# Seeding the fourth product's PSUM bank with a ScalarE copy of the first, and keeping the up-projection's weight sums in DRAM, in a one-layer convolution, scan and MLP trunk

## The chip, the cores and the metric

The kernel runs on one core of a Trainium2 chip. The time is what the device needs for one execution, in microseconds (us). Three runs of the kernel before gave a median of 2695.03 us (2694.9 to 2701.88). Five engines take part, each with an instruction stream of its own: TensorE (PE, with its weight loads listed as PEld), VectorE (DVE), ScalarE (ACT), GpSimd (POOL) and SyncE (SP). SP's stream issues nearly all of the kernel's transfers, one after the other. An engine works through its stream in order: an instruction that waits holds up whatever stands behind it.

## The reference

One layer works on x of shape (1, 2048, 1024) in float32. A normalisation and one input projection feed two mixers, a gated short convolution and a Mamba-2 state-space scan (SSD); an output projection and a squared-ReLU MLP with residual sums follow, then a last normalisation.

```python
h = rmsnorm(x, norm_mix_w)
proj = jnp.einsum("btd,dc->btc", h, w_in)
u_b, u_c, u_h, z, xbc, dt_raw = jnp.split(proj, SPLITS, axis=-1)
y_a = short_conv_mixer(u_b, u_c, u_h, short_conv_w)        # u_b * conv3(u_c * u_h)
y_b = ssd_mixer(z, xbc, dt_raw, ...)                       # conv4, silu, chunked scan, gate silu(z), rmsnorm
x = x + jnp.einsum("btc,cd->btd", jnp.concatenate([y_a, y_b], axis=-1), w_out)
h = rmsnorm(x, norm_mlp_w)
hid = jnp.square(jax.nn.relu(jnp.einsum("btd,df->btf", h, w_up)))
return x + jnp.einsum("btf,fd->btd", hid, w_down)
```

## The kernel before

**Three matmuls for one product.** Operands are float32. Each is split into a high part in the matmul format (`whi`, `uh`: a cast on ScalarE, L100 and L315) and the rest (`wlo`, `ul`: a subtraction on VectorE, L101 and L316). A product of 128x128 weights and 128x512 activations is three matmuls: high by high, high weights by low activations, low weights by high activations (L270, L271, L272).

**Seven products for eight.** The input projection, the MLP's up-projection and the down-projection multiply 2x2 blocks in the manner of Strassen and Winograd. A block multiplication is a *chain* (`Seven.chain`, L244 to L281) of seven products, in the order of the table `PRODUCTS`: b11, t1, t2, b21, t3, b22, t4. Each sums over four *places* (pieces of the contraction), so it is 12 matmuls, and a chain has 84. Activations stand ready as sums and differences of their blocks, split into high and low. The weights need three forms besides the first block: `s12` and `s34` (two halves each), formed on VectorE by four 128x512 additions or subtractions (`combine`, L223 to L242; they appear as L231 and L208), and the last block `a22`.

**Banks.** A product's result grows in a PSUM bank of 128x512. A chain has three by name: `px` takes b11 and, on top of it, t2, t3 and t4, each of which continues the sum (`start=False`); `py` takes t1 and then b22; `pw` takes b21 alone. `accs` sets how many buffers each kind has: 3 for px and py and 1 for pw in the projection, 4 and 2 in the MLP and the down-projection (L1533). After each product `evict` reads what the result needs: b11 alone belongs to the block c11 = b11 + b21, so before the change px is copied aside after b11 by ScalarE (`s1`, L689 in the projection, L835 in the MLP), and VectorE adds it to pw after b21 (`add`, L692 and L838). t1 and t2 are put aside in the same way (`s5`, `s2`) and added to what t3 and b22 give. While a copy of px is outstanding, t2 may not write on px.

**The stages.** Times are those of the trace.
- Input projection (`Proj`), first half of the positions: a start until about 200 us, then 20 chains until about 478 us. A pair of output columns has a kind: `z` (Silu on the result), `b` (multiplied by the convolution `cc`), `ch` and `x` (kept for the convolutions). This half forms the weight sums and stores `s12` and `s34` to DRAM (L234, L240). Its second half, about 478 to 965 us, has 22 chains, loads most of the sums from DRAM instead of forming them, and runs the scan on the side; the scan's instructions stand between those of the chains (L1206 to L1271).
- Output projection (`Output`), about 965 to 1411 us: 64 units of plain products; L1427 adds the residual. In its last units the MLP's first activations are loaded and split (`settle`, L314 to L316).
- MLP (`Mlp`), 16 chains on each half of the positions, about 1419 to 1742 us and to 2043 us. Each half loads the two weight blocks of a chain, `r0` and `r1` (512 KB each, tag `wraw`), and forms the sums anew. `relu2` (L841, L842) is a Relu and a Square on ScalarE; `store` writes the activations that the down-projection will need to `hid_d`.
- Down-projection (`down`, L953 to L981), about 2043 to 2640 us: chains listed in `STEPS`, one or two groups each, 35 groups in all. Every product is added on VectorE to an accumulator `acc` in SBUF (L969), which starts as the residual loaded from `x1_d`. `refill` loads the hidden activations back (`rh`) and splits them.
- The last three blocks and the norm, to the end.

**What sets the order.** The kernel is built with the Tile framework. Its scheduler decides in which order each engine's instructions stand; the code gives dependences, buffers and a sequence of calls. `chain` takes the next chain's weights from a generator `ahead`, one step after each product named in it, so that casts and sums for the next chain stand between the evictions of this one. Tags with a number of buffers (`wraw` 3, `whi` and `wlo` 4, `us` 2) decide how early a load or a split may begin.

Of the kernel before, what the change touches and what calls it, by code (L numbers as in the profile page):

```python
# [11 lines left out]
F32 = mybir.dt.float32  # L12
F32R = mybir.dt.float32r
AF = mybir.ActivationFunctionType
ALU = mybir.AluOpType

P = 128
# [6 lines left out]
KD = D // P  # L24
# [15 lines left out]
def trunk(ctx: ExitStack, tc: tile.TileContext, x, w_in, w_dt, w_out, w_up, w_down, cvec, hrow, out):  # L40
# [9 lines left out]
    accs = {}  # L50
# [139 lines left out]
    class Seven:  # L190
# [53 lines left out]
        def chain(self, groups, ws, ahead, evict, after):  # L244
# [3 lines left out]
            got = []  # L248
            PRODUCTS = (
                ("b11", 0, 0, "x", 1),  # L250
                ("t1", 1, 0, "y", 1),
                ("t2", 1, 1, "x", 0),
                ("b21", 0, 1, "w", 1),
                ("t3", 2, 0, "x", 0),
                ("b22", 2, 1, "y", 0),
                ("t4", 3, 0, "x", 0),
            )
            for name, wn, half, acc, first in PRODUCTS:
                at = half * n
                for gi, g in enumerate(groups):  # L260
                    if first:
                        tag = "mw" if acc == "w" else "mm"
                        pm[gi][acc] = psum(tag, "p" + acc, accs[tag])
                    p = pm[gi][acc]
                    i, j = WHERE[name]
                    for k, place in enumerate(g):
                        hi, lo = (t[:, (at + k) * P : (at + k + 1) * P] for t in ws[wn])
                        h = [t[:, j] for t in place[i]]
                        kw = dict(skip_group_check=not first)
                        nc.tensor.matmul(p, hi, h[0], start=bool(first and k == 0), stop=False, **kw)  # L270
# [3 lines left out]
                for gi in range(len(groups)):  # L274
                    evict(name, gi, pm[gi])
# [5 lines left out]
            return got  # L281

# [106 lines left out]
    class Proj(Seven):  # L389
# [272 lines left out]
        def pair(self, h, what, ws, ahead, after):  # L662
# [31 lines left out]
            def evict(name, gi, pm):  # L694
                if name == "b11":
                    copy(pm["x"], "s1")
# [4 lines left out]
                elif name == "b21":  # L701
                    add("c11", pm["w"], "s1")
# [6 lines left out]
                elif name == "b22":  # L709
                    add("c12", pm["y"], "s2")  # L710
                    if kind == "z":
                        nc.scalar.activation(a, a, AF.Silu)
                        nc.sync.dma_start(sz_d[h][:, n], a)
                    elif kind == "b":
                        mul(a, a, self.cc[n])
# [27 lines left out]
        def weights(self, h, what):  # L743

            if h == 0:
                sums_d[what] = dram.tile([P, 2, 1024], F32, name=f"sums_{what}_d")
                raws = self.load_cols(w_in, self.cols(what))()
                yield
                yield from self.combine(*raws, sums_d[what])
                return  # L750
            f0, f1 = self.cols(what)
            raw = lambda n, w=1024: wp.tile([P, 1024], F32, tag="wraw", name=n, bufs=3)[:, 0:w]
            r0 = load_w(w_in[f0])
            if what not in sums_d:
                r1 = load_w(w_in[f1])
                yield
                yield from self.combine(r0, r1)
                return
            s12, s34 = raw("s12"), raw("s34")
            nc.sync.dma_start(s12, sums_d[what][:, 0])  # L760
# [837 lines left out]
```

## Time and profile before

| what | value |
|---|---|
| median of three runs | 2695.03 us (2694.9 to 2701.88) |
| the profiled execution's span | 2694.2 us |
| what lies around the span, against the median | 0.8 us |
| TensorE busy | 2610.2 us, 12024 matmuls |
| VectorE busy | 1979.4 us, 2687 instructions |
| ScalarE busy | 1381.7 us, 2042 instructions |
| data moved | 522.27 MB, mean 194 GB/s |

By stage, TensorE's busy time is 277.6 of 278 us between 200 and 478 us (first half of the projection), 479.9 of 487 us in its second half, 431.2 of 446 us in the output projection, 319.8 of 332 us and 297.3 of 300 us in the two MLP halves, and 585.5 of 597 us in the down-projection. A matmul that follows another starts 0.227 us after it. Busy times count an instruction from its start to its end, and consecutive matmuls overlap, so their mean duration (0.39 us) is longer than the distance of their starts. A row such as "PE px L270 <- DVE e L838: 2.9, 2, 1.5" says that TensorE's instruction on px at L270 waited for VectorE's instruction at L838 for 2.9 us in all, twice, 1.5 us the longest time. In a timeline the bracket gives the idle time just before the instruction and what ended it.

### The profile page before, as it was taken

The page shows a single profiled execution, that of the slowest core. Times are in us where ns is not written, and L with a number is a line of the kernel's source. Part 1 is how long each engine was busy: PE and PEld are TensorE (multiplying, and loading weights), DVE is VectorE, ACT ScalarE, POOL GpSimd, SP SyncE. Part 2 cuts the span into 40 slices and gives each one's busy share as a digit, 9 for nine tenths or more (in the row PEclk, how much of TensorE's full clock was granted, in tenths as well). Part 3 has the DMA queues.
Part 4 walks back from the last instruction along what each step waited for, and adds up shares of the span by engine and source line. Part 5 has one row for each costly group of instructions (what it writes and reads, how often), then busy time and mean ns, then how long its engine had stood idle before and what let it go on. Part 6 is the DMA issues. An engine that isn't in the chain of part 4 may idle for free.

```text
span 2694.2 us, 33500 instructions
## 1 busy us (share of the span) xinstructions
PE 2610.2 (97%) x12024; PEld 2125.7 (79%) x12024; DVE 1979.4 (73%) x2687; ACT 1381.7 (51%) x2042; POOL 141.5 (5%) x162
## 2 busy tenths in 40 slices
PE   7999999999999999998999999999999999999998
PEld 5778888678887878776877788788887888888777
DVE  7997677667768766666658856765657887888985
ACT  6633345666567566757326445654545333334433
POOL 0000000011111001111000000000000000000001
PEclk9999999999999999999999999999999999999999
DMA  3575335555555588867596844644348544665752
GB/s 143 189 287 193 141 141 186 183 167 167 171 165 168 161 265 264 250 204 215 191 328 235 312 168 149 228 167 167 143 162 277 160 148 153 205 213 172 238 199 75
DMA packets 288262, 522.27 MB, mean 194 GB/s; under 512 B 25696, under 2 KB 141408, under 8 KB 288096
## 3 DMA queue, kind: packets, MB, share of 16 engines
q1 hardware_dynamic: 288096, 520.14, 57.8%
q8 instruction: 94, 1.54, 0.2%
q14 instruction: 72, 0.59, 0.1%
HBM read 349.65 MB, written 170.39 MB: 193 GB/s over the span
## 4 chain that ended last, share of the span: by engine, by line
PE 57%; issue 25%; DMA 7%; DVE 5%; ACT 3%; POOL 1%; SPq 1%; POOLq 0%; DVEq 0%; ACTq 0%
PE px L270 8%; PE px L272 8%; PE px L271 8%; PE py L270 4%; PE py L271 4%; PE py L272 4%; PE pm L113 3%; PE pm L114 3%; PE pm L115 3%; PE pw L270 2%; PE pw L272 2%; PE pw L271 2%; DMA dec<-rd_d 1%; DVE wlo L101 1%; PE yd L1243 1%
## 5 line engine op out<-in xcount | busy, mean ns | idle before, releaser
L270 PE MATMUL px<-uh,whi 128*128 128x512 f32 x1672 | 660.2, 395 | 27.3 <-DVE xt L1427 7.9
L272 PE MATMUL px<-uh,wlo 128*128 128x512 f32 x1672 | 654.1, 392 | 9.0 <-DVE wlo L101 9.0
L271 PE MATMUL px<-ul,whi 128*128 128x512 f32 x1672 | 653.9, 391 | 0.0
L270 PEld LDWEIGHTS px<-uh,whi 128*128 128x128 f32 x1672 | 315.7, 189 | 106.8 <-issue 16.4
L101 DVE TENSOR_TENSOR wlo<-wraw,whi 128x1024 fp32r<-128x1024 f32 x230 | 233.6, 1016 | 198.5 <-ACT whi L100 195.0
L272 PEld LDWEIGHTS px<-uh,wlo 128*128 128x128 f32 x1672 | 315.5, 189 | 78.3 <-DVE wlo L101 11.9
L271 PEld LDWEIGHTS px<-ul,whi 128*128 128x128 f32 x1672 | 315.9, 189 | 63.9
L100 ACT CAST whi<-wraw 128x1024 fp32r<-128x1024 f32 x230 | 203.1, 884 | 303.4 <-PE px L271 194.6
L100 ACT CAST whi<-s 128x1024 fp32r<-128x1024 f32 x210 | 219.2, 1044 | 226.8 <-PE py L271 89.9
L270 PE MATMUL py<-uh,whi 128*128 128x512 f32 x836 | 327.2, 391 | 2.2 <-ACT whi L100 2.2
L272 PE MATMUL py<-uh,wlo 128*128 128x512 f32 x836 | 325.7, 390 | 0.6 <-DVE wlo L101 0.5
L271 PE MATMUL py<-ul,whi 128*128 128x512 f32 x836 | 325.9, 390 | 0.0
L101 DVE TENSOR_TENSOR wlo<-s,whi 128x1024 fp32r<-128x1024 f32 x210 | 255.9, 1219 | 39.5 <-ACT whi L100 38.8
L113 PE MATMUL pm<-uh,whi 128*128 128x512 f32 (+1 forms) x648 | 252.9, 391 | 2.1 <-ACT uh L204 2.1
L114 PE MATMUL pm<-ul,whi 128*128 128x512 f32 (+1 forms) x648 | 249.1, 384 | 0.0
L115 PE MATMUL pm<-uh,wlo 128*128 128x512 f32 (+1 forms) x648 | 248.8, 384 | 0.0
L315 ACT CAST uh<-rh 128x1024 fp32r<-128x1024 f32 (+1 forms) x128 | 120.3, 944 | 144.2 <-PE py L272 123.0
L270 PEld LDWEIGHTS py<-uh,whi 128*128 128x128 f32 x836 | 156.9, 188 | 36.4 <-ACT whi L100 3.8
L272 PEld LDWEIGHTS py<-uh,wlo 128*128 128x128 f32 x836 | 156.9, 188 | 34.8 <-DVE wlo L101 1.9
L271 PEld LDWEIGHTS py<-ul,whi 128*128 128x128 f32 x836 | 157.0, 188 | 32.5 <-issue 0.2
L270 PE MATMUL pw<-uh,whi 128*128 128x512 f32 x418 | 163.6, 391 | 0.0
L272 PE MATMUL pw<-uh,wlo 128*128 128x512 f32 x418 | 163.2, 390 | 0.0
(215 smaller groups left out, 3798.8 us busy)
## 6 DMA issues: line engine op xcount, KB each, us to landing
hid_d<-e SPq DMA_DIRECT2D x96, 512.0 KB, 3.3
rh<-hid_d SPq DMA_DIRECT2D x96, 512.0 KB, 4.2
wraw<-w_in SPq DMA_DIRECT2D x68, 512.0 KB, 3.8
wraw<-w_up SPq DMA_DIRECT2D x64, 512.0 KB, 5.0
wraw<-w_down SPq DMA_DIRECT2D x104, 256.0 KB, 3.6
dec<-rd_d SPq DMA_DIRECT2D x32, 512.0 KB, 5.4
wraw<-w_out SPq DMA_DIRECT2D x32, 512.0 KB, 5.2
x_d<-xt SPq DMA_DIRECT2D x64, 256.0 KB, 3.7
```

Of the source, the lines that this page charges most:

```text
L100: nc.scalar.copy(hi, raw)
L101: eng.tensor_tensor(out=lo, in0=raw, in1=hi.bitcast(F32), op=ALU.subtract)
L113: nc.tensor.matmul(out, whi, hi, start=(k == 0), stop=False)
L114: nc.tensor.matmul(out, whi, lo, start=False, stop=False)
L115: nc.tensor.matmul(out, wlo, hi, start=False, stop=(k == nk - 1))
L270: nc.tensor.matmul(p, hi, h[0], start=bool(first and k == 0), stop=False, **kw)
L271: nc.tensor.matmul(p, hi, h[1], start=False, stop=False, **kw)
L272: nc.tensor.matmul(p, lo, h[0], start=False, stop=(k == len(g) - 1), **kw)
L315: nc.scalar.copy(p[i][0], t)
L1243: nc.tensor.matmul(yd[(i % 2) * 64 : (i % 2) * 64 + 64, (i // 2) * L : (i // 2 + 1) * L], byhead(t["xdt"])[:, i, :], t["dec"][:, i, :], st ...
```

## The change

There are two parts.

*The seed.* After b11, `chain` now asks for the bank `pw` at once and lets ScalarE copy px into it. b21 then continues the sum in pw instead of starting it, so that pw holds b11 + b21 when b21 is done. In the projection's `evict` nothing is put aside after b11 any more, and c11 comes straight out of pw: by Silu for z, by a multiplication with cc for b, by a ScalarE copy for ch and x; the later step on the whole width for z and b is now on the second half only. In the MLP `relu2` reads pw directly, and the second `relu2` is on 512 columns instead of 1024. In the down-projection the VectorE add of b11 is gone, and the add after b21 takes both. `accs["fresh"] = 2` leaves the first two groups after the banks of the MLP are opened unseeded: they go the old way.

*The stored sums.* `weights` of the projection becomes `pairs`, which the MLP now uses too (`sums_of`): the MLP's first half forms and stores `s12` and `s34` (two stores of 512 KB a chain), and its second half loads `r0`, `s12`, `s34` and, later, `a22` (256 KB) instead of `r0` and `r1`, and forms no sums.

```diff
             for name, wn, half, acc in PRODUCTS:
                 at = half * n
                 for gi, g in enumerate(groups):
-                    if first:
-                        tag = "mw" if acc == "w" else "mm"
-                        pm[gi][acc] = psum(tag, "p" + acc, accs[tag])
+                    seeded = acc in pm[gi]
+                    if not seeded:
+                        pm[gi][acc] = bank(acc)
...
-                        nc.tensor.matmul(p, hi, h[0], start=bool(first and k == 0), stop=False, **kw)
+                        nc.tensor.matmul(p, hi, h[0], start=not seeded and k == 0, stop=False, **kw)
...
                 for gi in range(len(groups)):
+                    if name == "b11" and gi >= fresh:
+                        pm[gi]["w"] = bank("w")
+                        nc.scalar.copy(pm[gi]["w"], pm[gi]["x"])
+                        seeds.add(gi)
                     evict(name, gi, pm[gi])
...
+        def pairs(self, w, cols, what, first):
+
+            f0, f1 = cols
+            r0 = load_w(w[f0])
+            if first or what not in sums_d:
+                r1 = load_w(w[f1])
+                yield
+                yield from self.combine(r0, r1, sums_d.get(what))
+                return
+            raw = lambda n, w=1024: wp.tile([P, 1024], F32, tag="wraw", name=n, bufs=3)[:, 0:w]
+            s12, s34 = raw("s12"), raw("s34")
+            nc.sync.dma_start(s12, sums_d[what][:, 0])
+            nc.sync.dma_start(s34, sums_d[what][:, 1])
+            yield
+            yield split_w(r0, nc.vector)
+            a22 = raw("a22", 512)
+            nc.sync.dma_start(a22.rearrange("p (k c) -> p k c", c=P), w[f1][:, KD // 2 :])
+            yield split_w(s12, nc.vector)
+            yield split_w(s34, nc.vector)
+            yield split_w(a22, nc.vector)
...
                 if name == "b11":
-                    copy(pm["x"], "s1")
+                    pass
...
                 elif name == "b21":
-                    add("c11", pm["w"], "s1")
+                    if kind == "z":
+                        nc.scalar.activation(to["c11"], pm["w"], AF.Silu)
+                    elif kind == "b":
+                        mul(to["c11"], pm["w"], self.cc[n][:, lo])
+                    else:
+                        nc.scalar.copy(to["c11"], pm["w"])
...
                 elif name == "b21":
-                    add(e0[:, 0], pm["w"], "s1")
+                    if gi in self.seeds:
+                        relu2(e0[:, 0], pm["w"])
+                    else:
+                        add(e0[:, 0], pm["w"], "s1")
+                        relu2(e0[:, 0], e0[:, 0])
...
                 elif name == "b22":
                     add(e0[:, 1], pm["y"], "s2")
-                    relu2(e0, e0)
+                    relu2(e0[:, 1], e0[:, 1])
...
+        def sums_of(self, h, q):
+            if h == 0:
+                sums_d[q] = dram.tile([P, 2, 1024], F32, name=f"sums_{q}_d")
+            return self.pairs(w_up, (2 * q, 2 * q + 1), q, h == 0)
...
                 if not last:
-                    ahead = self.weights(self.load_cols(w_up, (2 * q + 2, 2 * q + 3)))
+                    ahead = self.sums_of(h, q + 1)
...
                     t = self.acc[h, d][c]
+                    if name == "b11" and gi in self.seeds:
+                        return
                     nc.vector.tensor_tensor(out=t, in0=pm[p], in1=t, op=ALU.add)
...
-    accs.update(mm=4, mw=2, pool=c4.enter_context(tc.tile_pool(name="pw", bufs=1, space=PS, reuse_waits="tile")))
+    accs.update(mm=4, mw=2, fresh=2, pool=c4.enter_context(tc.tile_pool(name="pw", bufs=1, space=PS, reuse_waits="tile")))
```

The order of the instructions moves with it. In the changed kernel the lines are others: L274 to L276 are the three matmuls (L270 to L272 before), L344 and L345 the cast and subtraction of `settle` (L315 and L316), L1452 the residual add (L1427), and L281 is the seed copy.

VectorE at the start of the MLP, before: the low parts of the first chain's weights (`wlo`), of its activations (`ul`, from the loaded `rb`), and the residual add into `xt` that ends the output projection.

```order
L101 TENSOR_TENSOR wlo_11863<-s12_11859,whi_11862 128x1024
L101 TENSOR_TENSOR wlo_11907<-s34_11903,whi_11906 128x1024
L316 TENSOR_TENSOR ul0_11924<-rb_11881,uh0_11923 128x1024
L316 TENSOR_TENSOR ul0_11928<-rb_11883,uh0_11927 128x1024
L316 TENSOR_TENSOR ul0_11932<-rb_11885,uh0_11931 128x1024
L316 TENSOR_TENSOR ul0_11936<-rb_11887,uh0_11935 128x1024
L1427 TENSOR_TENSOR xt_11866<-pm_11910,xt_11866 128x512
L101 TENSOR_TENSOR wlo_11962<-wraw_11853,whi_11961 128x512
```

The same place on VectorE in the changed kernel:

```order
L101 TENSOR_TENSOR wlo_11823<-s12_11818,whi_11822 128x1024
L101 TENSOR_TENSOR wlo_11868<-s34_11863,whi_11867 128x1024
L345 TENSOR_TENSOR ul0_11885<-rb_11841,uh0_11884 128x1024
L345 TENSOR_TENSOR ul0_11889<-rb_11843,uh0_11888 128x1024
L1452 TENSOR_TENSOR xt_11826<-pm_11871,xt_11826 128x512
L345 TENSOR_TENSOR ul0_11893<-rb_11845,uh0_11892 128x1024
L101 TENSOR_TENSOR wlo_11923<-wraw_11812,whi_11922 128x512
L345 TENSOR_TENSOR ul0_11897<-rb_11847,uh0_11896 128x1024
```

The residual add has moved ahead of two of the four activation subtractions.

TensorE in the first chain of the down-projection, from the end of t1 (the last three matmuls on `py`) on, before:

```order
L270 MATMUL py_16854<-uh0_16624,whi_16671 128x512
L271 MATMUL py_16854<-ul0_16625,whi_16671 128x512
L272 MATMUL py_16854<-uh0_16624,wlo_16672 128x512
L270 MATMUL pw_16887<-uh1_16675,whi_16664 128x512
L271 MATMUL pw_16887<-ul1_16676,whi_16664 128x512
L272 MATMUL pw_16887<-uh1_16675,wlo_16665 128x512
```

And in the changed kernel:

```order
L274 MATMUL py_16833<-uh0_16602,whi_16649 128x512
L275 MATMUL py_16833<-ul0_16603,whi_16649 128x512
L276 MATMUL py_16833<-uh0_16602,wlo_16650 128x512
L274 MATMUL px_16818<-uh1_16653,whi_16649 128x512
L275 MATMUL px_16818<-ul1_16654,whi_16649 128x512
L276 MATMUL px_16818<-uh1_16653,wlo_16650 128x512
```

Before, b21 (on `pw`) went ahead of t2; now t2 (on `px`) follows t1, as the table `PRODUCTS` has it.

ScalarE at the boundary of two chains in the middle of the down-projection, before: casts of weights (`whi`) and of refilled activations (`uh`).

```order
L100 CAST whi_17317<-s34_17314 128x1024
L315 CAST uh3_17344<-rh_17325 128x512
L100 CAST whi_17340<-wraw_17233 128x512
L315 CAST uh0_17384<-rh_17362 128x1024
L100 CAST whi_17417<-wraw_17378 128x1024
```

The same place in the changed kernel:

```order
L100 CAST whi_17295<-s34_17292 128x1024
L344 CAST uh3_17322<-rh_17303 128x512
L100 CAST whi_17318<-wraw_17212 128x512
L281 COPY pw_17339<-px_17326 128x512
L344 CAST uh0_17363<-rh_17341 128x1024
L100 CAST whi_17395<-wraw_17357 128x1024
```

The seed copy stands between the cast of `a22`, which the chain before it still needs, and the next refilled activation's cast.

More of the change, by code (lines that the diff above doesn't have):

```diff
@@ L873, in half @@
                         pass
[L874 removed]
+                    ahead = self.sums_of(1, 0)
                 else:
@@ L1524, in trunk @@
             if n == 62:
-                ahead = mlp.weights(mlp.load_cols(w_up, (0, 1)))
+                ahead = mlp.sums_of(0, 0)
                 next(ahead)
```

53 lines of the change are left out of this document (18 added, 35 removed).

## The prediction

> **What bounds the kernel now.** I read the page first, then TensorE's busy time by stretches of 50 us, then what TensorE waits for, and then the instructions around each of its long waits. The page gives the span and who is busy:
>
> ```profile
> span 2694.2 us, 33500 instructions
> PE 2610.2 (97%) x12024; PEld 2125.7 (79%) x12024; DVE 1979.4 (73%) x2687; ACT 1381.7 (51%) x2042; POOL 141.5 (5%) x162
> ```
>
> TensorE (PE) is busy for 97%, and the change takes no matmul away, so it can win only where TensorE stands still or runs slowly. The stretches show where. Their columns: bounds, length, then busy time and instructions of PE, PE's weight load, VectorE (DVE), ScalarE (ACT) and GpSimd, the granted clock, DMA share, GB/s:
>
> ```profile
> 1400.00:1450.00 50.00, 40.50 (x167) 32.39 (x166) 36.96 (x43) 28.48 (x35) 0.00 (x0) 0.90 0.76 267
> ...
> 1500.00:1550.00 50.00, 47.33 (x197) 37.38 (x196) 37.79 (x55) 22.61 (x32) 0.00 (x0) 0.97 0.83 300
> 1550.00:1600.00 50.00, 50.00 (x222) 41.39 (x222) 29.43 (x38) 24.45 (x34) 0.00 (x0) 1.00 0.45 163
> 1700.00:1750.00 50.00, 48.65 (x213) 39.51 (x212) 40.85 (x50) 34.85 (x45) 0.00 (x0) 1.00 0.74 266
> 1750.00:1800.00 50.00, 48.60 (x214) 39.59 (x213) 32.52 (x45) 26.66 (x37) 0.00 (x0) 1.00 0.48 179
> ...
> 2050.00:2100.00 50.00, 44.19 (x179) 33.85 (x178) 38.88 (x59) 14.54 (x20) 0.00 (x0) 0.93 0.75 252
> ...
> 2500.00:2550.00 50.00, 48.37 (x212) 39.41 (x211) 46.40 (x64) 23.28 (x26) 0.00 (x0) 1.00 0.76 247
> ```
>
> A full stretch holds 222 matmuls, 0.225 us each. By that measure the others lose 55 x 0.225 = 12.4 us (MLP start), 5.6 (1500 to 1550), 2.0 + 1.8 (hand-over between the MLP's halves), 9.7 (MLP to down) and 2.3 us (late down). What TensorE waits for (total, times, longest):
>
> ```profile
> PE pst L131 <- DVE facc L454: 12.4, 1, 12.4
> PE px L272 <- DVE wlo L101: 9.0, 6, 3.1
> PE px L270 <- DVE xt L1427: 7.9, 1, 7.9
> PE pss L1268 <- DVE facc L1441: 7.0, 1, 7.0
> PE px L270 <- DVE acc L969: 6.4, 9, 1.3
> PE px L270 <- ACT whi L100: 6.3, 4, 2.6
> PE px L270 <- DVE e L838: 2.9, 2, 1.5
> PE px L270 <- ACT s L689: 1.4, 2, 1.2
> ```
>
> The first and fourth are sums of squares that the change does not touch. The rest, 34 us, is all that the chains wait for, and part of it is for transfers. So the reward is bounded at some 35 us with the slow matmuls behind waits; VectorE's saved time is not itself a gain.
>
> **The change part by part.** Durations first (busy total, mean ns, then idle before it):
>
> ```profile
> L689 ACT COPY s<-px 128x512 f32<-128x512 f32 x84 | 48.6, 578 | 32.1 <-PE px L272 32.1
> L1440 ACT ACTIVATE sq<-xt 128x512 f32<-128x512 f32 x14 | 8.4, 597 | 11.4 <-DVE xt L1427 11.4
> L838 DVE TENSOR_TENSOR e<-pw,s 128x512 f32<-128x512 f32 x32 | 22.1, 690 | 13.7 <-PE pw L272 13.7
> L969 DVE TENSOR_TENSOR acc<-px,acc 128x512 f32<-128x512 f32 x140 | 95.4, 688 | 41.6 <-PE px L272 37.8 <-DMA acc<-x_d 3.6
> L231 DVE TENSOR_TENSOR s<-wraw 128x512 f32<-128x512 f32 x84 | 58.0, 691 | 66.3 <-DMA wraw<-w_down 26.8 <-DMA wraw<-w_up 26.5 <-DMA wraw<-w_in 13.0
> L842 ACT ACTIVATE e<-e 128x512 f32<-128x512 f32 x64 | 40.5, 632 | 1.0
> L842 ACT ACTIVATE e<-e 128x1024 f32<-128x1024 f32 x32 | 34.0, 1061 | 0.8
> ```
>
> The trace has no copy from one PSUM bank to another. Nearest are ScalarE's read of a bank (L689, 0.578) and its write into one (L1440, 0.597); I take 0.58, and twice that as the upper bound if the two ports added. The copies stand in for SBUF copies in the projection and the MLP; only down's 35 and the ch and x pairs' second copies (28) are new work for ScalarE, 63 x 0.58 = 37 us. In the MLP two activations of 1061 become four of 632, 0.4 us a chain. VectorE loses about 72 adds from b21, 35 from b11 in down and 4 x 16 weight sums: 171 x 0.69 = 118 of 1979 us. Neither engine is the bound, so I cost both at nothing in the steady chains. The cover is t1: 12 x 0.225 = 2.7 us pass between b11's end and t2, which takes the copied bank next, and 5.4 us before b21, which needs the seed. A cast ahead of the copy adds at most some 1.0 us. If that cover fails, every late copy stalls TensorE by its excess.
>
> One rule speaks against the hand-over. The Trainium skill ("ScalarE: Activation LUTs", section "Rules for kernel authors") says to use VectorE, not ScalarE, for adds and relu, VectorE being up to about 3 times faster in bf16. If its factor held for these tiles, a copy would be some 2.1 us (an estimate from that page), and with a cast outlast t1 by 0.4 us, 107 times, 43 us slower; in the rows a ScalarE copy of such a bank is the shorter one, 0.578 against 0.688 us, so I give that outcome no chance.
>
> *MLP start.* TensorE's first matmul waits for the last residual add, which stands on VectorE behind four low-part subtractions (L316):
>
> ```profile
> 1413.85 4.63 DVE L316 TENSOR_TENSOR ul<-rb,uh 128x1024 fp32r<-128x1024 f32 x4
> 1418.39 0.69 DVE L1427 TENSOR_TENSOR xt<-pm,xt 128x512 f32<-128x512 f32 x1
> 1419.22 0.77 PE L270 MATMUL px<-uh,whi 128*128 128x512 f32 x1 [7.93 <-DVE xt L1427]
> 1419.78 0.63 PE L271 MATMUL px<-ul,whi 128*128 128x512 f32 x1
> 1420.21 0.63 PE L272 MATMUL px<-uh,wlo 128*128 128x512 f32 x1
> ```
>
> In the new order only two stand ahead: 2 x 1.16 = 2.3 us earlier. The 1.5 us wait for L838 that follows may go as well. But the next weights' loads still come after the first half's last normalised blocks, and 1500 to 1550 loses 5.6 us where those weights arrive late. An earlier start runs into that wait harder. I take 2 of the 3.8 us (-2 to 6).
>
> The matmuls here also run at 0.43 us from start to start, half pace, and the stretch's clock is 0.90. The MLP-to-down stretch shows 0.93, though its longest wait is 2.6 us (below). The Trainium skill ("TensorE: Matmul & The Clock Gate", section "Part 1: The HAM clock gate (the "warmup" mystery)") drops the clock to half only after an idle window of about 3.4 us; by that reading the waits of down's start would cost nothing beyond themselves, and of the 3.5 us that a clock of 0.93 is short over 50 us my sum would lose some 2 (an estimate from that page).
>
> *Between the MLP's halves.* VectorE waits for up weights before it can sum them, and t3's add stands behind:
>
> ```profile
> 1756.44 0.69 DVE L231 TENSOR_TENSOR s<-wraw 128x512 f32<-128x512 f32 x1 [3.46 <-DMA wraw<-w_up]
> 1757.05 0.69 DVE L838 TENSOR_TENSOR e<-px,s 128x512 f32<-128x512 f32 x1
> ```
>
> The second half loads its sums, so nothing of that kind stands on VectorE. Of the 3.8 us lost there I take 2.3 (1.4 to 3.3). The price is on the DMA side: half 0 stores 2 x 512 KB a pair, half 1 loads 1.75 MB instead of 1 MB. The stores are all on SP's queue, where the refill loads stand too; that is in the MLP start's lower end.
>
> *MLP to down.* In the old order b21 goes ahead of t2, because b11's bank is freed only by VectorE's add, and that waits for a transfer:
>
> ```profile
> PE px L272 <- DVE wlo L101: 2.6, 1, 2.6
> PE px L270 <- ACT whi L100: 2.1, 1, 2.1
> ...
> 2063.94 0.69 DVE L969 TENSOR_TENSOR acc<-px,acc 128x512 f32<-128x512 f32 x1 [1.31 <-DMA acc<-x_d]
> 2064.68 0.50 PE L270 MATMUL px<-uh,whi 128*128 128x512 f32 x1 [0.80 <-DVE acc L969]
> ```
>
> The seed copy frees the bank at once, so the 0.8 us goes, and t2's 2.7 us of work covers casts that TensorE stood for. The casts themselves (2.1 and 2.6) come from refills and may stay. Of 9.7 us I take 5 (2 to 7).
>
> *Down.* Nine waits for L969, 6.4 us. Those in which t2 waits for b11's add vanish, since no add is there any more; two examples, the first delayed by a weight sum that waited for its load:
>
> ```profile
> 2528.68 0.69 DVE L231 TENSOR_TENSOR s<-wraw 128x512 f32<-128x512 f32 x1 [1.61 <-DMA wraw<-w_down]
> 2529.89 0.68 DVE L969 TENSOR_TENSOR acc<-px,acc 128x512 f32<-128x512 f32 x1
> 2530.63 0.50 PE L270 MATMUL px<-uh,whi 128*128 128x512 f32 x1 [1.35 <-DVE acc L969]
> 2610.67 0.50 PE L270 MATMUL px<-uh,whi 128*128 128x512 f32 x1 [1.16 <-DVE acc L969]
> ```
>
> These two are 2.5 us. The other six, without the 0.8 of down's start, are 6.4 - 0.8 - 2.5 = 3.1 us of t3 and t4, whose adds stay and whose queue is only 0.7 us shorter a group. I take 3.5 with the slow first matmul behind each (2.5 to 6).
>
> *Projection.* At the hand-over of its halves TensorE waits 2.6 us for a cast; an add fewer ahead gives 1 (0 to 4). Against that, the second half's ch and x pairs put a copy more on ScalarE, where TensorE already waits 1.4 us for L689: -1.5 (-3 to 0).
>
> Sum: 2 + 2.3 + 5 + 3.5 + 1 - 1.5 = 12.3, about 12 us. The profiled execution's 2694.2 us becomes 2682; the 0.8 us that lie around the span bring the median of the runs from 2695.0 to 2683.
>
> **The rivals.**
>
> *Relief that reappears* (about -4, 2691). Every stall named ends in a transfer or a cast on refilled data. If those end at the same time as before, TensorE arrives earlier and waits longer; then only down's 2.5 us and about 1.5 of the others are left. The 5.6 us in the stretch from 1500 speak for it, the absence of transfers in down's two waits against it.
>
> *All of it* (-30, 2665). If VectorE's shorter queue releases every chain wait of the table but the 6.3 us on ScalarE's casts, 28 us go, with slow matmuls 30. Against it: L231 waits for down weights remain, and they hold t3's and t4's adds.
>
> *ScalarE's queue late* (+12, 2707), slower. In the projection's second half ScalarE holds instructions that wait for GpSimd:
>
> ```profile
> ACT stmp L1262 <- POOL y L1259: 58.9, 13, 8.7
> ```
>
> A seed behind one of those 13 waits (mean 4.5 us) ends after t1's 2.7 us and stalls t2 by 4.5 + 0.6 - 2.7 = 2.4 us; five hits are 12 us. It decides from the point where the seed ends over 2.7 us after b11. Before, t2 needed the copy L689 from the same place, and TensorE waited only twice for it, 1.4 us; that speaks against it. The extra copies and a bank copy at twice 0.58 us speak for it.
>
> That the change would not do what it says is out: the seeds stand in ScalarE's order in all chains but the first two of the MLP.
>
> **How the numbers follow.** Forecast (gain 6 to 22, its terms not all at one end): 0.53, 2683. Relief that reappears (0 to 8): 0.27. All of it: 0.10. ScalarE late: 0.10. A measurement of this kernel tells about 0.3%, 8 us, from no change. Faster by more: the forecast but for its lowest part, 0.53, and all of it 0.10, together 0.63; within: 0.27; slower: 0.10. The range, 2666 to 2698, leaves out half of the -30 case and most of the slower one.
>
> **What would show it.** Right: the stretches from 1400 and 2050 hold some 17 and 22 matmuls more (3.8 and 5 us), t2 follows t1 at down's start, no wait of t2 for L969's successor is left, no L231 wait for up weights in half 1, bank copies of 0.58 us. Wrong: new waits for the seed copy or for s copies in the projection's second half, a deeper loss after 1500, copies over 1 us, or VectorE's saved 118 us with the same counts of matmuls in every stretch.

## The result and the profile after

The changed kernel takes 2685.93 us (median of 4 runs, 2678.42 to 2686.92), the kernel before 2697.03 in the same comparison (2694.9 to 2701.88). The ratio is 0.995 with a 95% interval of 0.9933 to 0.9966: 11 us faster by the medians and 13 by the ratio, where 12 were forecast. The profiled spans are 2694.2 and 2685.2 us, 9.0 apart. The total agrees, but the places do not: the gain came largely from where none was forecast, and a loss stands where a small gain was.

The page of the changed kernel, its span and busy times:

```profile
span 2685.2 us, 33606 instructions
...
PE 2608.8 (97%) x12024; PEld 2126.4 (79%) x12024; DVE 1876.7 (70%) x2524; ACT 1431.9 (53%) x2176; POOL 147.9 (6%) x162
```

VectorE works 103 us less, where 118 were counted, and ScalarE 50 us more, as counted (37 for the copies and 13 in the MLP). The same stretches as before the change, in the same columns:

```profile
1400.00:1450.00 50.00, 38.14 (x147) 28.60 (x147) 38.58 (x46) 30.13 (x40) 0.00 (x0) 0.86 0.81 277
1450.00:1500.00 50.00, 49.82 (x220) 40.93 (x219) 46.42 (x64) 30.30 (x45) 0.00 (x0) 1.00 0.91 330
1500.00:1550.00 50.00, 44.11 (x183) 35.46 (x182) 31.19 (x45) 20.85 (x31) 0.00 (x0) 0.93 0.87 327
1750.00:1800.00 50.00, 50.00 (x222) 41.41 (x221) 23.02 (x28) 27.06 (x41) 0.00 (x0) 1.00 0.73 263
2050.00:2100.00 50.00, 44.92 (x183) 35.79 (x182) 38.05 (x56) 15.63 (x21) 0.00 (x0) 0.93 0.74 248
2500.00:2550.00 50.00, 49.54 (x219) 40.71 (x218) 45.41 (x61) 24.98 (x28) 0.00 (x0) 1.00 0.74 235
```

The MLP's start is worse: 147 matmuls where there were 167, and 183 where there were 197; between 1450 and 1550 the DMA rate has risen from 273 and 300 to 330 and 327 GB/s. MLP to down (2050) hardly moved, 183 after 179; the hand-over between the halves and late down are better. These stretches are fixed in time, while the MLP now begins 10 us earlier; the count by stage below allows for that. What TensorE waits for now:

```profile
PE px L274 <- DVE xt L1452: 7.7, 1, 7.7
...
PE px L274 <- ACT whi L100: 6.4, 2, 5.5
...
PE px L274 <- DVE e L851: 3.7, 4, 2.1
PE py L274 <- DVE acc L994: 3.5, 1, 3.5
...
PE px L276 <- DVE wlo L101: 2.2, 3, 1.5
...
PE px L274 <- ACT pw L281: 1.6, 2, 1.4
...
PE pw L274 <- ACT pw L281: 1.4, 2, 0.7
...
PE px L274 <- DVE acc L994: 1.2, 2, 0.8
```

Of down's nine waits of px for VectorE's add two are left, and waits for low weights fell from 9.0 to 2.2 us. New are a wait of 5.5 us for a weight cast, one of 3.5 us for t1's add on py, and 3.0 us of waits for the seed (L281).

For a count by stage I took, from the trace, the time by which the start of a matmul follows the start of the one before it by more than 0.227 us, for all distances above 0.25 us, and summed it by stage. The MLP's stages are counted from the last matmul of the output projection in each trace (1410.9 before, 1400.7 after): to 36 us behind it, to 150, to 320, to 356, to 628, to 670, and down from there to 2650 us of the span. The scan's small matmuls count in it, the same in all columns. The stages that the table leaves out, from 150 to 320 us and from 356 to 628, lose at most 1.4 us in these five kernels.

| lost, us | before | after | seed alone | sums alone | seed in projection alone |
|---|---|---|---|---|---|
| start, 60 to 200 us | 12.3 | 5.3 | 5.9 | 13.4 | 6.0 |
| hand-over of the projection, 468 to 548 | 11.0 | 6.6 | 6.5 | 9.3 | 6.5 |
| MLP's start, first 36 us | 12.3 | 14.7 | 10.1 | 10.2 | 10.9 |
| MLP's start, 36 to 150 us | 5.5 | 11.4 | 1.2 | 12.8 | 3.0 |
| between the MLP's halves | 3.7 | 0.5 | 4.9 | 1.7 | 3.0 |
| MLP to down | 9.5 | 9.8 | 5.2 | 14.6 | 12.5 |
| down | 8.1 | 3.1 | 4.5 | 9.2 | 7.0 |

Each column is one profiled execution. From MLP to down, the last column's kernel works in nearly the same way as the one before, and they differ by 3 us there, so a difference of 3 us between single executions tells little. What is said below rests on the medians, and on differences in the table that are larger or that several kernels show.

### The profile page after: what moved, and what is told of

Read it like the earlier page. It is cut to its first block, busy times and chain, and to the rows that moved or that the text cites. A ratio compares the mean times of both kernels' runs of the same rounds, so it can differ in the third digit from the quotient of the medians.

```text
span 2685.2 us, 33606 instructions
## 1 busy us (share of the span) xinstructions
PE 2608.8 (97%) x12024; PEld 2126.4 (79%) x12024; DVE 1876.7 (70%) x2524; ACT 1431.9 (53%) x2176; POOL 147.9 (6%) x162
## 5 line engine op out<-in xcount | busy, mean ns | idle before, releaser
L274 PE MATMUL px<-uh,whi 128*128 128x512 f32 x1672 | 660.3, 395 | 23.3 <-DVE xt L1452 7.7
L276 PE MATMUL px<-uh,wlo 128*128 128x512 f32 x1672 | 653.7, 391 | 2.2 <-DVE wlo L101 2.2
L274 PEld LDWEIGHTS px<-uh,whi 128*128 128x128 f32 x1672 | 315.4, 189 | 101.1 <-issue 9.5
L101 DVE TENSOR_TENSOR wlo<-wraw,whi 128x1024 fp32r<-128x1024 f32 x214 | 223.7, 1045 | 227.5 <-ACT whi L100 221.7
L276 PEld LDWEIGHTS px<-uh,wlo 128*128 128x128 f32 x1672 | 315.4, 189 | 70.4 <-DVE wlo L101 3.8
L100 ACT CAST whi<-wraw 128x1024 fp32r<-128x1024 f32 x214 | 193.5, 905 | 316.1 <-PE px L275 205.6
L274 PE MATMUL py<-uh,whi 128*128 128x512 f32 x836 | 327.8, 392 | 4.7 <-DVE acc L994 3.5
L276 PE MATMUL py<-uh,wlo 128*128 128x512 f32 x836 | 325.9, 390 | 0.0
L274 PEld LDWEIGHTS py<-uh,whi 128*128 128x128 f32 x836 | 157.5, 188 | 39.3 <-DVE acc L994 3.9
L276 PEld LDWEIGHTS py<-uh,wlo 128*128 128x128 f32 x836 | 157.2, 188 | 33.1 <-DVE wlo L101 0.2
L274 PE MATMUL pw<-uh,whi 128*128 128x512 f32 x418 | 163.6, 391 | 1.4 <-ACT pw L281 1.4
L276 PE MATMUL pw<-uh,wlo 128*128 128x512 f32 x418 | 162.7, 389 | 0.0
L275 PE MATMUL pw<-ul,whi 128*128 128x512 f32 x418 | 162.7, 389 | 0.0
```

The costliest lines, as they stand in the source:

```text
L100: nc.scalar.copy(hi, raw)
L101: eng.tensor_tensor(out=lo, in0=raw, in1=hi.bitcast(F32), op=ALU.subtract)
L274: nc.tensor.matmul(p, hi, h[0], start=not seeded and k == 0, stop=False, **kw)
L275: nc.tensor.matmul(p, hi, h[1], start=False, stop=False, **kw)
L276: nc.tensor.matmul(p, lo, h[0], start=False, stop=(k == len(g) - 1), **kw)
```

## The experiments

The baseline in each comparison is the kernel before, run in the same set; its median was 2694.8 to 2696.2 us in them.

**The two halves of the change.** First the seed alone:

```diff
         def sums_of(self, h, q):
-            if h == 0:
-                sums_d[q] = dram.tile([P, 2, 1024], F32, name=f"sums_{q}_d")
-            return self.pairs(w_up, (2 * q, 2 * q + 1), q, h == 0)
+            return self.weights(self.load_cols(w_up, (2 * q, 2 * q + 1)))
```

> The seed as in the changed kernel, the up weight sums formed anew in both halves. Theory (the stored sums' stores on SP's queue delay the up weights at the MLP's start and cost some 8 us there, and save 3 between the halves): 5 us below the changed kernel, about 14 us below before; the stretch from 1405 to 1560 us loses 18 us as before, the hand-over between the halves 3 to 4. Rival (the seed's earlier start of the MLP runs into the same weights later): about the time of the changed kernel or above it, 26 us lost in that stretch here too.

Measured: 2673.36 us, ratio 0.9922 (0.9907 to 0.9938), 22 us below before and 13 below the changed kernel. That is the theory's direction, and more than its number. Its waits of TensorE in the stretch from 1390 to 1560 us, and in the changed kernel from 1400 to 1560:

```profile
PE px L274 <- DVE xt L1450: 7.9, 1, 7.9
PE pw L274 <- ACT pw L281: 0.7, 1, 0.7
```

```profile
PE px L274 <- DVE xt L1452: 7.7, 1, 7.7
PE px L274 <- ACT whi L100: 6.4, 2, 5.5
PE px L274 <- DVE e L851: 2.2, 2, 2.1
PE px L274 <- ACT s L848: 0.7, 1, 0.7
PE px L275 <- DVE ul L345: 0.5, 1, 0.5
PE px L276 <- DVE wlo L101: 0.4, 1, 0.4
```

Without stored sums only the first wait and one seed are left. Then the sums alone, the kernel before with the generator `pairs` and its calls in the MLP:

```diff
                 if not last:
-                    ahead = self.weights(self.load_cols(w_up, (2 * q + 2, 2 * q + 3)))
+                    ahead = self.sums_of(h, q + 1)
```

> The kernel before with the up weight sums stored by its first half and loaded by its second, no seed. Theory: 5 us slower than before: 8 us more lost at the MLP's start, 3 less between the halves. Rival (the MLP's start loses by the seed): 3 us faster than before, 18 us lost at the MLP's start as before.

Measured: 2710.38 us, ratio 1.006 (1.0044 to 1.0076), 15 us slower. The loss at the MLP's start is there without any seed, as the table shows, so it isn't the seed's. The seed's 22 us less the sums' 15 would be 7 where the change gains 11 to 13, so the two effects don't simply add.

**Where the seed's gain lies.** The seed in the projection only:

```diff
-    accs.update(mm=4, mw=2, fresh=2, pool=c4.enter_context(tc.tile_pool(name="pw", bufs=1, space=PS, reuse_waits="tile")))
+    accs.update(mm=4, mw=2, fresh=1000, pool=c4.enter_context(tc.tile_pool(name="pw", bufs=1, space=PS, reuse_waits="tile")))
```

with `sums_of` as in the first experiment. (The MLP's Relu and Square stay in two halves, as in the changed kernel.)

> The seed in the input projection alone; MLP and down-projection put b11 aside as before, sums formed anew. Theory: the projection's gain is all there, 7 us in its first 200 us and 4 at the hand-over of its halves, so about 10 us below before; down's 8 us of loss as before. Rival (the start's 7 us is chance of one execution): 3 us below before, 12 us lost between 60 and 200 us.

Measured: 2688.46 us (12 runs), ratio 0.9967 (0.9954 to 0.998), 7 us below before by the medians and 9 by the ratio. The start's 12 us are 5.3 to 6.4 in every kernel that seeds the projection by ScalarE once and 13.4 in the one that does not seed, so this is no chance of one execution. The rest of the seed's 22 us, 12 by the ratios and 15 by the medians, lies in the MLP and in down.

**Who copies.** The seed alone, copied by VectorE:

```diff
-                        nc.scalar.copy(pm[gi]["w"], pm[gi]["x"])
+                        nc.vector.tensor_copy(pm[gi]["w"], pm[gi]["x"])
```

> The seed alone (sums formed anew in both halves), with the seed copied by VectorE instead of ScalarE. Theory (the gain is VectorE's relief where its queue is full: the first 200 us, the hand-over, down): most of the 22 us goes, the first 200 us lose 11 to 13 us again, down 8; about 10 us or less below before. Rival (the gain comes from the add that no longer stands between b21 and what reads it, whoever copies): within 4 us of the seed alone.

Measured: 2721.67 us, ratio 1.0095 (1.0076 to 1.0114): 48 us above the seed alone and 27 above the kernel before. Both expectations fell short. VectorE's stream and TensorE's wait around one seed, and the sum of such waits in this kernel:

```profile
174.10 1.29 DVE L208 TENSOR_TENSOR nb<-nb 128x512 f32<-128x512 f32 x2
175.30 0.70 DVE L281 COPY pw<-px 128x512 f32<-128x512 f32 x1
```

```profile
176.05 0.79 PE L274 MATMUL px<-uh,whi 128*128 128x512 f32 x1 [7.70 <-DVE pw L281]
```

```profile
PE px L274 <- DVE pw L281: 23.2, 9, 7.7
PE py L274 <- ACT s L718: 13.7, 12, 2.5
```

VectorE works without a break from 167 us on convolution and normalisation, and t2 waits 7.7 us for the seed. The copy's length (0.694 us in this kernel, 0.573 on ScalarE) explains little of the 48 us: if all 107 copies were waited for to their end, the difference would be 13. The rest is the copy's place in a full queue.

**How well the copy is covered.** The seed alone, every copy made twice:

```diff
-                        nc.scalar.copy(pm[gi]["w"], pm[gi]["x"])
+                        for _ in range(2):
+                            nc.scalar.copy(pm[gi]["w"], pm[gi]["x"])
```

> The seed alone with every seed copy made twice, so that a copy costs 1.16 instead of 0.58 us. Theory (t1's 2.7 us cover the copy): within 4 us of the seed alone, although ScalarE works 61 us more. Rival (the copies lie on the path): each chain's t2 waits 0.58 us longer, 60 us slower than the seed alone; if only those behind other waits on ScalarE do, 0.58 us at the four or five places where the trace shows a wait for the seed, 3 us.

Measured: 2685.38 us, ratio 0.9968 (0.9956 to 0.998), 12 us above the seed alone, for 61 us more work on ScalarE. So four fifths are covered and one fifth is not; none of the three numbers expected was that. TensorE's waits for the seed, first in the seed alone, then with two copies:

```profile
PE px L274 <- ACT pw L281: 6.6, 4, 3.0
```

```profile
PE px L274 <- ACT pw L282: 13.1, 11, 3.3
```

Four waits become eleven, so a part of the chains has less than 0.6 us to spare. The loss in the scan half (548 to 965 us) goes from 13.6 to 19.3 us in the count by stage.

**What the stored sums cost.** The changed kernel with sums stored and loaded from the sixth pair on only:

```diff
-            if h == 0:
+            if h == 0 and q >= 5:
                 sums_d[q] = dram.tile([P, 2, 1024], F32, name=f"sums_{q}_d")
```

> The changed kernel, but only the sums of up weight pairs 5 to 15 are stored and loaded; pairs 0 to 4, whose stores would fall into the MLP's start, are formed anew in both halves. Theory: the 8 us at the MLP's start are gone, the 3 between the halves come back: 5 us below the changed kernel, the same as with the seed alone. Rival (any loading of sums in the second half costs by its transfers): no better than the changed kernel.

Measured: 2675.07 us, ratio 0.9929 (0.9914 to 0.9945): the first five pairs carry all of the cost, and the other eleven pairs gain nothing over the seed alone (2673.36). Then the stores issued by ScalarE:

```diff
-        def combine(self, r0, r1, kept=None):
+        keeper = nc.sync
+
+        def combine(self, r0, r1, kept=None, by=None):
...
-                nc.sync.dma_start(kept[:, 0], s12)
+                by.dma_start(kept[:, 0], s12)
...
-                nc.sync.dma_start(kept[:, 1], s34)
+                by.dma_start(kept[:, 1], s34)
...
-                yield from self.combine(r0, r1, sums_d.get(what))
+                yield from self.combine(r0, r1, sums_d.get(what), self.keeper)
...
     class Mlp(Seven):
         stored = hn_d
+        keeper = nc.scalar
```

> The changed kernel with the MLP's stores of the sums issued by ScalarE, right after the sum that the next cast waits for anyway, instead of by SP. Theory (a store that waits for VectorE's sum holds SP's queue, and the up weights' loads behind it): the 8 us that the changed kernel loses more at the MLP's start go, so 8 us below the changed kernel, near the seed alone. Rival (the transfers themselves crowd the DMA engines, or the loads stand late in SP's order whoever issues the stores): no gain, 26 us lost between the MLP's start and 150 us behind it.

Measured: 2685.05 us, ratio 0.9966 (0.9952 to 0.9979), the changed kernel's time. That speaks against my theory that stores waiting on SP hold up the loads behind them; but ScalarE has the waits now, and its casts stand behind them, so the tiny stores below are the cleaner answer. Next, all sums stored, none read:

```diff
+            if h == 1:
+                return self.weights(self.load_cols(w_up, (2 * q, 2 * q + 1)))
             return self.pairs(w_up, (2 * q, 2 * q + 1), q, h == 0)
```

> The changed kernel with the MLP's first half storing all its sums, but the second half forming them anew (the stored sums are not read). Theory (the stores are what costs, in the first half): 15 us lost more than with the seed alone between the MLP's start and 150 us behind it, as in the changed kernel, and 4 us between the halves as with the seed alone; 2686 to 2690 us. Rival (the loads of the second half cost, too, at the end of the MLP): 8 us below the changed kernel.

Measured: 2687.68 us, ratio 0.9965 (0.9949 to 0.9981). It loses 14.5 + 11.3 us at the MLP's start, as the changed kernel does. So the stores cost. Reading them back in the second half changes the time by less than the runs can tell: 5.3 us lost between the halves instead of 0.5, and 4.3 at MLP to down instead of 9.8. Then the same stores with nearly no bytes:

```diff
+        cut = 1024
...
+            cut = self.cut
...
-                nc.sync.dma_start(kept[:, 0], s12)
+                nc.sync.dma_start(kept[:, 0, 0:cut], s12[:, 0:cut])
...
-                nc.sync.dma_start(kept[:, 1], s34)
+                nc.sync.dma_start(kept[:, 1, 0:cut], s34[:, 0:cut])
...
     class Mlp(Seven):
         stored = hn_d
+        cut = 16
```

> The same, but each store takes only 16 of 1024 columns: as many stores on SP with the same waits for VectorE, nearly no bytes, and the up weights' loads stand in SP's order about where they do with the seed alone. If the stores' waits in SP's queue cost: as slow as with full stores. If the bytes, or the places of the loads that follow from them, cost: within 4 us of the seed alone, 2673 us.

Measured: 2674.27 us, ratio 0.992 (0.9899 to 0.9941), the seed alone's time. As many stores with the same waits cost nothing, so the theory of waits on SP falls. And bytes without stores, added to the seed alone:

```diff
             self.store(h, q, e0, e1, e2)
+            if h == 0:
+                t = dram.tile([P, 1024], F32, name=f"extra_{q}_d")
+                nc.gpsimd.dma_start(t, hid_d[h][q][:, 0:2].rearrange("p a t -> p (a t)"))
             return got
```

> The seed alone, and for each chain of the MLP's first half a copy of 512 KB from DRAM to DRAM, issued by GpSimd: 1 MB read and written, what the two stores of a chain move, with SP's order and buffers left as they are with the seed alone. If the bytes themselves cost: 10 us or more lost between the MLP's start and 150 us behind it, 2683 us or more. If the places of the loads in SP's order cost: within 4 us of the seed alone.

Measured: 2681.92 us, ratio 0.9946 (0.9926 to 0.9966), 8.6 us above the seed alone. Here one of the loads stands ahead of the third block's stores (`hn_d`) in SP's order, as in the seed alone, so extra bytes cost by themselves. But they do not cost where the changed kernel loses. In the count by stage this run loses 15.3 us in the MLP's first 150 us, against 11.3 in the seed alone and 26.2 in the changed kernel, and 9.0 us between 150 and 320, where those two lose 0.4 and 1.1. What waits is different, too. VectorE's first sum on the up weights between 1400 and 1745 us, in the seed alone, in this run and in the changed kernel:

```profile
L231 DVE TENSOR_TENSOR s<-wraw 128x512 f32<-128x512 f32 x18 | 12.4, 686 | 10.3 <-DMA wraw<-w_up 10.3
```

```profile
L231 DVE TENSOR_TENSOR s<-wraw 128x512 f32<-128x512 f32 x17 | 11.7, 686 | 21.0 <-DMA wraw<-w_up 21.0
```

```profile
L231 DVE TENSOR_TENSOR s<-wraw 128x512 f32<-128x512 f32 x16 | 11.1, 691 | 11.2 <-DMA wraw<-w_up 11.1
```

With the extra copies VectorE stands 10.7 us longer for up weights; in the changed kernel it doesn't. Nor are the copies as heavy as the stores: between 1400 and 1550 us the rate is 279 GB/s in the seed alone, 292 with the copies and 311 in the changed kernel.

The changed kernel's longest new wait there is the 5.5 us for a weight cast. Its weights are loaded late. In the seed alone a load stands ahead of the third block's stores:

```profile
1487.04 0.78 SPq L95 DMA_DIRECT2D wraw<-w_up  x1
1490.01 2.17 SPq L402 DMA_DIRECT2D hn_d<-nb  x3
```

In the changed kernel, and with all sums stored but not read, the next load stands behind them, and ScalarE's cast waits for it:

```profile
1501.64 3.32 SPq L402 DMA_DIRECT2D hn_d<-nb  x3
...
1512.10 0.91 SPq L95 DMA_DIRECT2D wraw<-w_up  x2
```

```profile
1519.17 1.04 ACT L100 CAST whi<-wraw 128x1024 fp32r<-128x1024 f32 x1 [3.12 <-DMA wraw<-w_up]
```

The order changes with the stores' size alone: with the tiny stores the load is ahead. How long those loads take between 1400 and 1550 us, in the seed alone, with tiny stores, and in the changed kernel (last column: median us from issue to landing; with the extra copies it is 5.9):

```profile
wraw<-w_up SPq DMA_DIRECT2D x16, 512.0 KB, 5.0
```

```profile
wraw<-w_up SPq DMA_DIRECT2D x17, 512.0 KB, 4.8
```

```profile
wraw<-w_up SPq DMA_DIRECT2D x14, 512.0 KB, 6.9
```

The last run takes the loads off SP: the changed kernel with the blocks r0 and r1 loaded by GpSimd.

```diff
-    def load_w(src):
+    def load_w(src, by=nc.sync):
         raw = wp.tile([P, 1024], F32, tag="wraw", name="wraw", bufs=3)
-        nc.sync.dma_start(raw.rearrange("p (k c) -> p k c", k=src.shape[1]), src)
+        by.dma_start(raw.rearrange("p (k c) -> p k c", k=src.shape[1]), src)
...
-            r0 = load_w(w[f0])
+            r0 = load_w(w[f0], self.loader)
...
-                r1 = load_w(w[f1])
+                r1 = load_w(w[f1], self.loader)
...
     class Mlp(Seven):
         stored = hn_d
+        loader = nc.gpsimd
```

> The changed kernel with the up weights' loads issued by GpSimd, which is idle in the MLP, so that no load stands behind the stores of the normalised blocks on SP. If the place in SP's order costs: the 15 us at the MLP's start go and the 4 us saved between the halves stay, 2669 to 2673 us, the best of all. If the bytes cost: 2683 to 2688 us, as the changed kernel.

Measured: 2688.78 us, ratio 0.9973 (0.996 to 0.9987). No gain on the whole, and the loads' median time is 6.9 us here, too. But by stage the loads' places do matter. The MLP's first 150 us lose 18.3 us instead of 26.2, and the wait of 5.5 us for a weight cast is gone (0.9 now). In its place 5.3 us are lost in the last 50 us of the output projection, where no other kernel loses anything, and 5.1 instead of 0.5 between the halves. TensorE's wait at the end of the output projection (1350 to 1420 us), and its wait for a weight cast on px between 1420 and 1560 us:

```profile
PE pm L113 <- DVE xt L1455: 3.4, 1, 3.4
```

```profile
PE px L276 <- ACT whi L100: 0.9, 1, 0.9
```

The first is for a residual add of VectorE at 1377.4 us. VectorE had stood still for 6.2 us until 1359.9, for an up weight that GpSimd loads, and is behind from there on; that this is what delays the add is likely, not shown.

So this much is shown: the cost comes with the stores of the first five pairs, and with their full size, not with their number or their waits. How much of it is the traffic and how much the places that the loads get in SP's order stays open. The full stores bring both, the extra copies bring traffic and cost 8.6 us elsewhere, and the run without SP takes the places away and gets back 7.9 us at the MLP's start, which it loses again elsewhere. Nor do the runs tell whether the DMA engines or the memory behind them is what the bytes fill.

**Down's start.** The seed alone with the first column's residual blocks loaded by GpSimd:

```diff
-                nc.sync.dma_start(t[n], x1_d[h * NBB + bb][:, d + i])
+                (nc.sync if h or d else nc.gpsimd).dma_start(t[n], x1_d[h * NBB + bb][:, d + i])
```

> The seed alone with the residual blocks of down's first output column loaded through GpSimd's queue instead of SP's, where the loads stand behind eleven weight and refill transfers. Theory (at MLP to down the seed's gain is held back by t1's add, which waits for these loads): 2 us below the seed alone, no wait for VectorE's add at down's start. Rival (the loads wait for the buffers of the MLP's last result to be stored, whatever the queue): the same time as the seed alone.

Measured: 2672.89 us, ratio 0.9916 (0.9899 to 0.9933), the same as the seed alone. TensorE's wait for t1's add goes on (1.05 us against 1.80 in the two traces), so the queue isn't what delays these blocks. The trace agrees: GpSimd has nothing else to do there and still issues three of the four only at 2040.90 us, after a wait of 26.3 us for VectorE, where SP issued its loads of these blocks from 2040.58 on. That they wait for the buffers fits this, and was not tried by itself.

The seed alone takes 0.9922 of the time before, against 0.995 with both parts. No run is faster than it by more than the intervals.

## Why the prediction came out as it did

*The total* was right, 2685.93 against 2683, for a sum whose terms were not. By experiment the seed gives 22 us and the stored sums take 8 (by the ratios) to 13 (by the medians) of them back; the prediction gave some 10 to the seed's terms and 2 to the sums'. By stage, the projection gave some 10 us more than forecast, the MLP's start 10 less and MLP to down 5 less. That these nearly cancel is luck.

*The projection* was the largest miss on the gain's side: -0.5 forecast (1 for the hand-over, -1.5 for the late copies), about 10 measured, since the output projection's last matmul comes at 1400.7 instead of 1410.9 us. The step that failed is that the start before 200 us got no term: "Neither engine is the bound, so I cost both at nothing in the steady chains", and the start, which is not steady, was not looked at apart. These stretches of the kernel before show VectorE over 90% busy while TensorE stands:

```profile
100.00:150.00 50.00, 48.41 (x214) 39.53 (x213) 45.70 (x55) 22.93 (x29) 2.30 (x3) 1.00 0.60 218
150.00:200.00 50.00, 43.27 (x179) 33.77 (x178) 46.54 (x59) 21.72 (x25) 4.46 (x8) 0.97 0.83 299
```

TensorE waits there mostly for low weights, which VectorE forms. The row between 60 and 200 us, before and after:

```profile
PE px L272 <- DVE wlo L101: 5.1, 3, 3.1
```

```profile
PE px L276 <- DVE wlo L101: 1.8, 2, 1.5
```

With an add less on VectorE in each chain, the 12.3 us lost become 5.3; with the seed on VectorE they are 19.1. The hand-over gave 4.3 us, just past the bound of "0 to 4".

*The MLP's start* was forecast at 2 us gained and lost 8.3 (17.8 to 26.2). The order's part was right: the residual add stands behind two subtractions, and TensorE waits 7.7 us, from an earlier time. The step that failed reads "The price is on the DMA side: ... that is in the MLP start's lower end", 2 us slower at most. What the runs show in its place is a cost of 8 to 13 us for the stores. The first five pairs' stores, 5 MB where 270 to 300 GB/s already moved, carry it; whether by their traffic, by the place that a load gets behind other stores, or by both was not separated. It should have been priced by that stretch's weights, which already landed late: the 5.6 us from 1500 stood in the table. The seed alone turns these 5.5 into 1.2, so the fear that an earlier start only waits harder was wrong.

*Between the halves* 2.3 was forecast, and 3.3 measured; the wait of VectorE's sum for up weights is gone, as said. At *MLP to down* 5 were forecast and nothing was measured. In the six kernels that form the sums anew and seed the MLP by ScalarE the loss there is 4.3 to 7.4 us (9.5 before); in the four that load stored sums at the end it is 7.8 to 9.8. So the loads probably take the gain back here, but single executions differ by 3 us at this place, and it was not shown by a run of its own. The mechanism holds (t2 now follows t1) but what is late next was not named:

```profile
2061.72 0.69 DVE L994 TENSOR_TENSOR acc<-py,acc 128x512 f32<-128x512 f32 x1 [0.65 <-DMA acc<-x_d]
```

```profile
2062.47 0.80 PE L274 MATMUL py<-uh,whi 128*128 128x512 f32 x1 [3.51 <-DVE acc L994]
```

b22 continues on py behind t1's add, and that waits for the residual of c22. This is the rival "relief that reappears", at this one place.

*Down* was right in place and mechanism, 5.0 us for 3.5: no t2 waits for an add any more. It loses 3.1 to 5.2 us in the nine kernels whose ScalarE makes one seed copy there, and 7.0 to 9.2 in the three that don't seed down.

*ScalarE late* did appear, as 3.0 us of waits for the seed, longest 1.4, one of them in the scan half; five hits of 2.4 us did not come. In the seed alone these waits are 7.9 us, the longest 3.0 at the end of the MLP's first half. The run with two copies shows how near it is. The copy itself took 0.573 us, where 0.58 was taken from its neighbours. The Trainium skill's rule to use VectorE for adds and relu ("ScalarE: Activation LUTs", section "Rules for kernel authors") gives its factor for bf16 and does not name copies; for this float32 copy between PSUM banks the runs show the opposite: it is shorter on ScalarE, and moving it to VectorE costs 48 us.

## What to carry to other kernels

A busy share is to be read by stage for the engine that is relieved as well as for the bound: 73% over the span hid 94% between 50 and 200 us (140.4 of 150), and there the adds removed were time gained. Bytes that replace arithmetic are priced in the stretch in which they move: if its loads already land late, a store that nobody waits for can still delay those that are waited for. And a step handed to another engine is worth what that engine's queue is short at that point; the same copy gained 22 us on ScalarE and lost 27 on VectorE.

## What the runs showed of the hardware

A copy between PSUM banks of 128x512 float32 takes 0.573 us on ScalarE (107 in the profile) and 0.694 on VectorE.

Half pace after a pause does not follow the pause's length alone. After 1.88 us (the kernel with extra copies) matmuls started 0.43 us apart, and after 3.13 us (the kernel with late sums) 0.23:

```profile
1668.57 0.50 PE L274 MATMUL px<-uh,whi 128*128 128x512 f32 x1 [1.88 <-DVE e L851]
...
1669.65 0.63 PE L274 MATMUL px<-uh,whi 128*128 128x512 f32 x1
1670.08 0.63 PE L275 MATMUL px<-ul,whi 128*128 128x512 f32 x1
```

```profile
1731.74 0.50 PE L274 MATMUL px<-uh,whi 128*128 128x512 f32 x1 [3.13 <-ACT pw L281]
...
1732.54 0.39 PE L274 MATMUL px<-uh,whi 128*128 128x512 f32 x1
1732.77 0.40 PE L275 MATMUL px<-ul,whi 128*128 128x512 f32 x1
```

All 22 pauses of 4.6 us or more before a matmul on px in these traces were followed at once by half pace; of the 38 between 1.5 and 3.5 us, 12 were at once and 4 more within the next seven matmuls. The Trainium skill ("TensorE: Matmul & The Clock Gate", section "Part 1: The HAM clock gate (the "warmup" mystery)") names an idle window of some 3.4 us, free-running, as what halves the clock; a window that starts at its own times fits the scatter, but pauses of little more than half its length were enough here. In the kernel before, the matmuls behind the wait of 2.56 us at down's start started 0.43 us apart, so the prediction was right not to price down's start by that page.
